# Score products of two heads (or of a differential head's two parts) issued in one step, in turn, each into a bank of its own

## The chip, the cores and the metric

The kernel runs on one core of one Trainium2 chip. The metric is the device time of one execution in microseconds, the median of three runs. A core has five engines that work through their own queues: PE (TensorE, matmuls; its weight loads are listed as PEld), DVE (VectorE), ACT (ScalarE), POOL (GpSimd) and SP, which only issues transfers here.

## What is computed

Three blocks in a row on x [256 tokens, 1024]: a block with a Fourier mixer, a convolution and 16 experts; a block with two attentions (eight heads with a compressed, a selected and a window branch, and eight plain causal heads); and two layers of four four-head mixers, each with a feed-forward part. The change concerns attention scores alone. Cut to those:

```python
# block 2: selected and window branch of nsa_attention, then moba_attention (256 tokens: causal, with ALiBi)
s = jnp.einsum('bgpqd,bgkd->bgpqk', qc, kwin) * scale - sl * dist
p = masked_softmax(s, mask)
o_win = jnp.einsum('bgpqk,bgkd->bgpqd', p, vwin)
# block 3, per layer: neighborhood, dilated and differential attention (latent attention has no pairs here)
s = jnp.einsum('bqhd,brqchd->bqhrc', q_row, k_nb) * scale + bias
s = jnp.einsum('bqhcd,bkhcd->bchqk', q_blk, k) * scale + bias[None, None]   # c: the two parts of a differential head
p = jax.nn.softmax(s, axis=-1)
a = p[:, 0] - lam * p[:, 1]
```

All sums are in float32. Heads are 64 wide, the parts of a differential head 32.

## The kernel before

The big products (`proj`, `proj_piece`, lines 147 to 149) have the tokens as stationary operand and 512 weight columns as moving one. A weight is split into a rounded part (ACT, line 99) and a rest (DVE, line 100), and three products per 128 rows, each in one pass, go into a bank of the pool `mm`. A projection keeps two of that pool's five banks, one for each half of the tokens, until ACT or DVE has read them.

The attentions are side work: generators that `pump` runs by a step or, with `rate` 2, by two steps between pieces of the projections. `pipeline` makes a step of three things: the score products and softmax of item i (`st1`), the transposes of the probabilities of item i - 2 (`st2`, lines 1077 and 1372), and the products with v of item i - 3 (`st3`, lines 1092, 1094, 1398, 1546). An item is one head, in block 2 one head of one branch, in the differential mixer one part of a head.

In `st1` of block 2 `scores` takes a bank of `mm`, makes the two causal halves (128 queries by 128 keys, line 1055; 128 queries by 256 keys, line 1056) and the softmax on them: DVE adds the bias and takes the maximum (line 1061), ACT the exponential (1065), DVE scales (1070). In the mixers `qk` (line 1360) makes two products of 128 queries by 256 keys, and `softmax` follows (1344 to 1354). The operands of a score product lie on 64 partitions: those of an even head on 0 to 63, those of an odd one on 64 to 127. A differential head's two parts lie on 32 partitions each. So two heads that follow each other use different rows of the PE array, but in this kernel their products stand in different steps.

A scheduler fixes the order of each engine's instructions when the program is built, and a tile waits for a free buffer of its pool.

Of the kernel before, what the change touches and what calls it, by code (L numbers as in the profile page):

```python
# [29 lines left out]
def row_bc(src, n):  # L30
    """A [n] DRAM vector seen by all partitions."""
    return bass.AP(src.tensor, src.offset, [[0, P], [1, n]])


class Net:
# [28 lines left out]
    def hT(self, tag, dt=F32R):  # L64
        """One of the two [128, 8, 256] tiles that carry a phase's transposed input."""
        return self.hp.tile([P, 2048], dt, tag=tag, name=tag).rearrange("p (k t) -> p k t", t=S)
# [4 lines left out]
    def load(self, dst, src):  # L71
        """The loads on this queue go out in the order that they are written down in."""
# [6 lines left out]
    def slot(self, dt=F32):  # L79
        """The next tile of the loads' rings."""  # L80
        pool, tag = self.rings[self.ring_at % len(self.rings)]
        self.ring_at += 1
        return pool.tile([P, 2064 if tag == "a8" else 2048], dt, tag=tag, name="wr")

    def load_rows(self, src):
        """The rows of src [k * 128, n] as [128, k tiles, n], in loads of up to 2048 columns; yields (first k tile, view)."""
# [15 lines left out]
    def behind(self, ins):  # L102
        """The next weights that are split wait on DVE behind ins."""
        self.held = [ins] * 3

    def split_to(self, t, raw):
        """Weights split into the two halves of a tile."""
# [15 lines left out]
    def proj(self, xh, xl, loads, n, evac, ahead=0):  # L123
        """out[half][128, n] = sum over k; loads are (first k tile, raw view [128, k tiles, n]). The first half of the rows
        takes the last pieces, ahead in number, before the second one does."""
# [27 lines left out]
    def queued(self):  # L153
        """The products of this block go out behind the last one that was noted, whichever is ready first."""
# [3 lines left out]
    def table(self, func, after):  # L158
        """Has the activation function's table in place before the data is; after [128, 1] is the last user of another one."""
        self.nc.scalar.activation(self.cp.tile([P, 1], F32, tag="warm", name="warm"), after, func)  # L160

    # Side work goes between the pieces of the projections: generators, run a step at a time in order.
# [4 lines left out]
    def soon(self, f):  # L167
        """Ahead of the other side work: one such closure per step."""
# [8 lines left out]
    def step(self):  # L177
        """A step of the first task, and of the next ones while the steps are light."""
# [7 lines left out]
    def finish(self, gen=None):  # L186
        """Emits side work up to the end of gen, or all of it."""
# [5 lines left out]
    def proj_cols(self, xh, xl, w, c0, n, evac, ahead=0):  # L193
        """Column chunk [c0, c0 + n) of a weight."""
# [9 lines left out]
    def rstd(self, ms, n, d, name, pool=True):  # L204
        """(ms / d + eps) ** -0.5 on [128, n] sums of squares: a power on Pool, or Newton steps on DVE where Pool is busy."""
# [11 lines left out]
        # Newton steps r (3 - t r r) / 2, with the factors -1/2 put off to the end  # L217
# [7 lines left out]
    def sumsq(self, x, n, name, ss=None):  # L225
        """Sums of squares over the last axis of x [128, 2, n], into ss [128, 2]."""
# [7 lines left out]
    def transpose_to(self, src, kts, consume, k0=0):  # L234
        """src [128 tok, 2, kts * 128] -> consume(kt, n, bank [128, n, 256]) for pairs of kt from k0 on."""
# [29 lines left out]
    def input_T(self, gain, name):  # L265
        """The residual stream as the next phase's input: its rows' rstd, and x^T * gain split in two, by column
        halves as they come. The rows' rstd is applied to the products, not to x."""
# [12 lines left out]
class InputT:  # L280
# [6 lines left out]
    def columns(self, c, soon=False):  # L287
        """Column half c; soon: its transposes go between the next projection's pieces."""
# [18 lines left out]
def gate_row(N, dst, src, j0, off):  # L307
    """dst[p, :] = mod[off:off + 1024] for every p, from column tiles j0, j0 + 1 of src, plus b_ada."""
# [10 lines left out]
def block1(N, stop):  # L319
    nc, a, tc = N.nc, N.a, N.tc  # L320
    x = N.x
    with ExitStack() as ctx:
# [29 lines left out]
        def ada_out(g, acc):  # L352
            """acc: rows 0, 32, 64, 96 hold the four 512-column blocks of c @ w_ada's group g."""
# [10 lines left out]
        def ada(g):  # L364
            """Weighted sum of the k tiles first, in steps that go between the projections, then one sum over partitions."""
# [38 lines left out]
        def shift_scale(c):  # L404
            """Shift and scale for k tiles 4 c .. 4 c + 3, a load per step, then the block's input with them."""
            accs, sbs, pt = [N.bank(N.po), N.bank(N.mm)], [], N.bank(N.tr)

            def columns(i):
                # the four partial sums, rows 0, 32, 64 and 96 of columns, become one column of rows
# [37 lines left out]
        # the first two chunks take their first k tiles while the second half of shift and scale is on its way  # L447
# [128 lines left out]
        for c in range(2):  # L576
            cc = slice(c * 512, c * 512 + 512)

            def ev(h, p, cc=cc):
# [7 lines left out]
                # the router's input, as it comes  # L587
# [8 lines left out]
class Router:  # L596
    """softmax(h2 @ w_router + b_router) with h2 = x * rstd * (g (1 + scale)) + shift: the affine part goes into the
    weights and a bias row, rstd onto the products."""
# [31 lines left out]
    def gate_rows(self):  # L630
        """gate_f's two halves on the partitions that hold them in the experts' outputs."""
# [7 lines left out]
    def squares(self, c, h):  # L639
        """Column half c of a half of the rows."""  # L640
# [31 lines left out]
    def second(self):  # L672
        """In an order in which the tensor engine has work while the last columns of x come."""
# [18 lines left out]
def moe(N, stop):  # L692
    nc, a, tc = N.nc, N.a, N.tc
    x, ident, rt = N.x, N.ident, N.router
    with ExitStack() as ctx:
        pool = ctx.enter_context(tc.tile_pool(name="moe1", bufs=1))
        N.m2 = ctx.enter_context(tc.tile_pool(name="m2m", bufs=1))
        # the ring goes on, with block 1's row tiles put in where they are free
# [29 lines left out]
        # the CAP largest are replaced, of equal ones the first; slots count up in order of index, 0 means not chosen  # L728
# [16 lines left out]
        # the chosen rows of x * rstd, exact in two parts, transposed; then the affine part of h2  # L745
# [29 lines left out]
        def out(n):  # L775
            """x + gate_f * moe for a column half: its sums of squares, the next input, then x = that * g_final and its sums."""
# [1015 lines left out]
```

## Time and profile before

| | |
|---|---|
| median of 3 runs | 2105.45 us |
| lowest, highest | 2105.32, 2109.12 us |
| the profiled execution, first to last instruction | 2108.0 us |
| block 2's eight heads with branches | about 1264 to 1340 us |
| block 2's eight plain heads | about 1364 to 1405 us |
| mixers of the two layers | about 1478 to 1573 us and 1807 to 1905 us |

The profile has no time for the execution besides its span, 2108.0 us. It gives the busy time of each engine by slice and by window, the chain of waits that ended last, groups of instructions by line, and the instructions in order of time. A PE record holds the pipeline's latency, so records overlap: what a product costs is the distance from its start to the next one's. A float32 product leaves two records (two passes), a product of the projections one.

### The profile page before, as it was taken

How to read it: one execution, taken by the hardware profiler on the slowest of the kernel's cores; microseconds unless marked ns; L12 is line 12 of the kernel's file. 1: busy time of each engine (PE TensorE's matmuls, PEld its weight loads, DVE VectorE, ACT ScalarE, POOL GpSimd, SP SyncE). 2: the span in 40 equal slices, each digit the busy share in tenths (PEclk: the TensorE clock that was granted, in tenths of full speed). 3: DMA queues.
4: the chain of work that ended last, by engine and by line, in shares of the span. 5: the costliest groups of instructions: out<-in, count | busy, mean ns of one | idle time of the engine just before them, and what ended most of it. 6: DMA issues, size and time to landing. Idle time of an engine off the chain costs nothing.

```text
span 2108.0 us, 22814 instructions
## 1 busy us (share of the span) xinstructions
PE 1756.7 (83%) x8895; PEld 1002.8 (48%) x8895; DVE 819.4 (39%) x1563; ACT 603.7 (29%) x1074; POOL 181.9 (9%) x135
## 2 busy tenths in 40 slices
PE   7989786566666666666666899999999999999998
PEld 4767631110110111111100487777778888778886
DVE  4797610000000000000000356676775545786554
ACT  4545410000000000000000345445545445455443
POOL 0671100000000000000000131112010000110000
PEclk9999897877777777766777899999999999999999
DMA  9879699999999999999999773336325556516551
GB/s 363 351 287 348 242 386 422 422 423 422 421 424 424 421 422 423 422 423 420 424 424 423 281 275 120 130 124 210 123 94 183 180 180 207 162 52 198 193 171 70
DMA packets 174396, 616.02 MB, mean 292 GB/s; under 512 B 11336, under 2 KB 20744, under 8 KB 139216
## 3 DMA queue, kind: packets, MB, share of 16 engines
q1 hardware_dynamic: 170288, 601.21, 73.4%
q0 software_dynamic: 3568, 12.75, 1.9%
q8 instruction: 70, 1.15, 0.2%
q10 hardware_dynamic: 432, 0.60, 0.1%
q14 instruction: 38, 0.31, 0.0%
HBM read 613.45 MB, written 4.24 MB: 293 GB/s over the span
## 4 chain that ended last, share of the span: by engine, by line
PE 51%; DMA 41%; DVE 5%; ACT 1%; issue 1%; POOL 0%; POOLq 0%; SPq 0%; DVEq 0%; ACTq 0%
DMA wr<-w_gate_e_dram 14%; DMA wr<-w_up_e_dram 14%; PE pb L147 13%; PE pb L148 13%; PE pb L149 13%; DMA wr<-w_down_e_dram 13%; PE pb L814 2%; DVE wl L100 2%; PE pb L242 2%; PE pb L1360 2%; PE pb L1372 1%; PE po L1398 1%; PE pb L760 1%; PE pb L1056 0%; PE pb L1055 0%
## 5 line engine op out<-in xcount | busy, mean ns | idle before, releaser
L100 DVE TENSOR_TENSOR wl<-wr,wh 128x1024 fp32r<-128x1024 f32 (+1 forms) x380 | 416.3, 1106 | 259.5 <-ACT wh L99 258.8
L814 PE MATMUL pb<-wr,XT 128*32 128x512 f32 x2048 | 362.8, 801 | 183.2 <-DMA wr<-w_up_e_dram 108.6
L99 ACT CAST wh<-wr 128x1024 fp32r<-128x1024 f32 (+1 forms) x380 | 340.0, 897 | 337.0 <-PE pb L149 313.1
L147 PE MATMUL pb<-wh,hh 128*128 128x512 f32 (+3 forms) x992 | 392.2, 396 | 1.8 <-ACT wh L99 1.2
L148 PE MATMUL pb<-wl,hh 128*128 128x512 f32 (+3 forms) x992 | 379.7, 383 | 6.6 <-DVE wl L100 6.5
L149 PE MATMUL pb<-wh,hl 128*128 128x512 f32 (+3 forms) x992 | 379.3, 383 | 0.0
L814 PEld LDWEIGHTS pb<-wr,XT 128*32 128x32 f32 x2048 | 47.9, 122 | 480.7 <-DMA wr<-w_up_e_dram 273.9
L857 PE MATMUL pb<-wr,hT 128*32 128x512 f32 x1024 | 186.7, 807 | 90.4 <-DMA wr<-w_down_e_dram 82.9
L828 DVE TENSOR_TENSOR hs<-pb,hs 128x512 f32<-128x512 f32 x16 | 11.1, 692 | 573.7 <-PE pb L814 573.7
L147 PEld LDWEIGHTS pb<-wh,hh 128*128 128x128 f32 x992 | 189.7, 191 | 50.0 <-issue 12.7
L148 PEld LDWEIGHTS pb<-wl,hh 128*128 128x128 f32 x992 | 189.8, 191 | 43.4 <-DVE wl L100 11.3
L149 PEld LDWEIGHTS pb<-wh,hl 128*128 128x128 f32 x992 | 189.3, 191 | 34.7
L827 ACT ACTIVATE hs<-pb 128x512 f32<-128x512 f32 x16 | 9.6, 598 | 543.9 <-PE pb L814 543.9
L857 PEld LDWEIGHTS pb<-wr,hT 128*32 128x32 f32 x1024 | 30.4, 127 | 229.3 <-DMA wr<-w_down_e_dram 194.6
L860 DVE TENSOR_TENSOR Y<-pb,gfr 128x512 f32<-128x512 f32 (+1 forms) x17 | 11.8, 692 | 269.1 <-PE pb L857 269.1
L841 ACT COPY Sc<-pb 128x256 f32<-128x256 f32 x16 | 6.0, 373 | 324.8 <-PE pb L839 324.8
L788 POOL TENSOR_TENSOR x<-x,grow 128x512 f32<-128x512 f32 x4 | 5.1, 1285 | 913.0 <-ACT jk L231 913.0
L147 PE MATMUL pb<-wh,ah 128*128 128x512 f32 x176 | 69.9, 397 | 0.0
L148 PE MATMUL pb<-wl,ah 128*128 128x512 f32 x176 | 69.6, 395 | 0.0
L149 PE MATMUL pb<-wh,al 128*128 128x512 f32 x176 | 69.6, 395 | 0.0
L864 PE MATMUL acc<-Y,Sc 64*128 64x512 f32 x128 | 45.9, 813 | 15.3 <-DVE Y L860 15.3
L1353 ACT ACTIVATE sb<-sb,cm 128x256 f32<-128x256 f32 x64 | 32.1, 503 | 40.5 <-DVE cm L1350 40.5
(505 smaller groups left out, 1794.3 us busy)
## 6 DMA issues: line engine op xcount, KB each, us to landing
wr<-w_gate_e_dram SPq DMA_DIRECT2D x128, 1024.0 KB, 19.6
wr<-w_up_e_dram SPq DMA_DIRECT2D x128, 1024.0 KB, 19.7
wr<-w_down_e_dram SPq DMA_DIRECT2D x128, 1024.0 KB, 19.6
wr<-w_in_dram SPq DMA_DIRECT2D x62, 1024.0 KB, 7.9
wr<-w_ada_dram SPq DMA_DIRECT2D x24, 1024.0 KB, 12.2
wr<-w_gate_dram SPq DMA_DIRECT2D x22, 1024.0 KB, 5.1
wr<-w_up_dram SPq DMA_DIRECT2D x22, 1024.0 KB, 5.1
wr<-w_down_dram SPq DMA_DIRECT2D x20, 1024.0 KB, 5.0
```

Of the source, the lines that this page charges most:

```text
L99: self.nc.scalar.copy(hi, src)
L100: self.nc.vector.tensor_tensor(lo, src, hi.bitcast(F32), ALU.subtract)
L147: nc.tensor.matmul(o, xh[:, kt, tok], hv[:, k, :], start=kt == first, stop=False)
L148: nc.tensor.matmul(o, xh[:, kt, tok], lv[:, k, :], start=False, stop=False)
L149: self.last_mm = nc.tensor.matmul(o, xl[:, kt, tok], hv[:, k, :], start=False, stop=kt == last).ins
L242: self.nc.tensor.transpose(pv[:, j, h * P:(h + 1) * P], src[:, h, (k + j) * P:(k + j + 1) * P], self.ident)
L760: nc.tensor.matmul(pg, part[:, h, k * P:(k + 1) * P], G[:, h, es].rearrange("p e c -> p (e c)"), start=(h == 0 and i == 0), stop=(h == 1 a ...
L814: N.last_mm = nc.tensor.matmul(pacc[32 * j:32 * j + 32, :], XT[:, k + kk, e, :], wt[:, kk, j * 512:(j + 1) * 512], start=(k + kk == 0), st ...
L857: nc.tensor.matmul(py[32 * q:32 * q + 32, :], hT[:, b, 32 * j:32 * j + 32], wt[:, i, n * 512 - c0:n * 512 - c0 + 512], start=(j == 0 and b ...
L864: nc.tensor.matmul(acc[n][h], Sc[r, h * P:(h + 1) * P], Y[r, :], start=(e == 0), stop=(e == NE - 1))
L1353: nc.scalar.activation(sb[:, c], (ps if bias is None else sb)[:, c], AF.Exp, bias=mm[:, h:h + 1], accum_out=sm[:, h:h + 1])
L1360: nc.tensor.matmul(ps[:, h * S:(h + 1) * S], q[:, h * P:(h + 1) * P], k, start=True, stop=True, tile_position=tile_position)
```

## The change

`scores` and `qk` take the operands of two items. They take a bank for each and issue the first product of the one, the first of the other, then the second of each. In block 2 the product with 256 keys now stands first. `st1` of an even item makes the products of the pair and keeps both banks; the odd item's step finds its scores there and only does the softmax. The latent mixer, whose heads lie on partitions 0 to 95 alone, keeps one head at a time. Comments were taken out too, so line numbers shift.

```diff
-        def scores(q, k, bias, gate):
-            ps = N.bank(N.mm)
-            nc.tensor.matmul(ps[:, :P], q[:, :P], k[:, :P], start=True, stop=True)
-            nc.tensor.matmul(ps[:, P:384], q[:, P:], k, start=True, stop=True)
+        def scores(heads):
+            ps = [N.bank(N.mm) for _ in heads]
+            for p, (q, k) in zip(ps, heads):
+                nc.tensor.matmul(p[:, P:384], q[:, P:], k, start=True, stop=True)
+            for p, (q, k) in zip(ps, heads):
+                nc.tensor.matmul(p[:, :P], q[:, :P], k[:, :P], start=True, stop=True)
+            return ps
+
+        def softmax(ps, bias, gate):
...
-                self.sb[i] = scores(self.q(n), self.k(s, n), self.bias[j], self.gate and self.gate(s, n))
+                if j == 0:
+                    self.ps[i], self.ps[i + 1] = scores([(self.q(m), self.k(s, m)) for m in (n, n + 1)])
+                self.sb[i] = softmax(self.ps.pop(i), self.bias[j], self.gate and self.gate(s, n))
...
-        def qk(q, k, tile_position=None):
-            ps = N.bank(N.mm)
+        def qk(*heads):
+            ps = [N.bank(N.mm) for _ in heads]
             for h in range(2):
-                nc.tensor.matmul(ps[:, h * S:(h + 1) * S], q[:, h * P:(h + 1) * P], k, start=True, stop=True, tile_position=tile_position)
+                for p, (q, k, *pos) in zip(ps, heads):
+                    nc.tensor.matmul(p[:, h * S:(h + 1) * S], q[:, h * P:(h + 1) * P], k, start=True, stop=True,
+                                     tile_position=pos[0] if pos else None)
             return ps
...
-                sb, sm = softmax(qk(*qk_of(n)), bias and bias(n))
+                if n % together == 0:
+                    for m, ps in enumerate(qk(*(qk_of(n + m) for m in range(together)))):
+                        pss[n + m] = ps
+                sb, sm = softmax(pss.pop(n), bias and bias(n))
...
-                sms[i] = softmax(qk(tv(df[0])[r, n // 2, :], tv(df[1])[r, n // 2, :], (r.start, 0)), tb[:, n])
+                if c == 0:
+                    pss[i], pss[i + 1] = qk(part(i), part(i + 1))
+                sms[i] = softmax(pss.pop(i), tb[:, n])
```

What moves on PE, first in block 2, at a step of an odd head. The rows name a line, the bank written (`pb`, `po`), the operands read (`wh`, `wl` a weight's two parts, `hh`, `hl` the input's, `sb` probabilities, `kT`, `qa` keys and queries) and the output's shape. Before, the odd head's scores stand between the transposes and the projection:

```order
L149 MATMUL pb<-wh,hl 128x512
L1077 MATMUL pb<-ident,sb 128x128 x3
L1055 MATMUL pb<-kT,qa 128x128
L1056 MATMUL pb<-kT,qa 128x256
L147 MATMUL pb<-wh,hh 128x512
```

The same step after the change:

```order
L149 MATMUL pb<-wh,hl 128x512
L1084 MATMUL pb<-ident,sb 128x128 x3
L147 MATMUL pb<-wh,hh 128x512
L148 MATMUL pb<-wl,hh 128x512
L149 MATMUL pb<-wh,hl 128x512
```

The odd head's two score products have left this place. They now stand at the even head's step (lines 1099 and 1101 are the products with v), which reads:

```order
L149 MATMUL pb<-wh,hl 128x512
L1099 MATMUL po<-pT,vr 64x256 x2
L1101 MATMUL po<-pT,vr 64x128 x2
L1084 MATMUL pb<-ident,sb 128x128 x3
L1057 MATMUL pb<-kT,qa 128x256 x2
L1059 MATMUL pb<-kT,qa 128x128 x2
L147 MATMUL pb<-wh,hh 128x512
```

There each score line stands twice, once per head and bank, where it stood once before. The second place is the differential mixer of the first layer, on PE (`df` are its queries and keys, `mr` the latent mixer's values). Before, two parts stand in two steps:

```order
L242 MATMUL pb<-ident,rows 128x128 x4
L1398 MATMUL po<-pT,mr 64x256 x4
L1360 MATMUL pb<-df 128x256 x2
L1372 MATMUL pb<-ident,sb 128x128 x4
L1360 MATMUL pb<-df 128x256 x2
L147 MATMUL pb<-wh,hh 128x512
```

After the change:

```order
L242 MATMUL pb<-ident,rows 128x128 x4
L1411 MATMUL po<-pT,mr 64x256 x4
L1371 MATMUL pb<-df 128x256 x4
L1384 MATMUL pb<-ident,sb 128x128 x4
L147 MATMUL pb<-wh,hh 128x512
```

The two parts' four products stand in a row, and one place where score products begin and end is gone. Over the whole program the score products of block 2 stand at 12 places in place of 24. In a layer, the differential mixer's stand at 4 in place of 9, the neighborhood's at 2 in place of 3, and the dilated mixer's at 3 in place of 4: its second pair stays apart, one head and then the other, as before.

## Rows read from the trace of the kernel before

**Rows 1.** The page's parts 1 (busy us by engine) and 4 (chain).

```profile
PE 1756.7 (83%) x8895; PEld 1002.8 (48%) x8895; DVE 819.4 (39%) x1563; ACT 603.7 (29%) x1074; POOL 181.9 (9%) x135
...
PE 51%; DMA 41%; DVE 5%; ACT 1%; issue 1%; POOL 0%; POOLq 0%; SPq 0%; DVEq 0%; ACTq 0%
```

**Rows 2.** Busy us by window: engine (instructions), granted clock, DMA share, GB/s.

```profile
1264.00:1340.00 76.00, 75.79 (x380) 53.98 (x378) 53.07 (x172) 39.56 (x93) 12.73 (x7) 1.00 0.34 111
1364.00:1405.00 41.00, 41.00 (x197) 28.55 (x196) 31.77 (x93) 19.40 (x47) 9.24 (x5) 1.00 0.34 116
1405.00:1420.00 15.00, 15.00 (x75) 12.11 (x75) 12.87 (x18) 7.34 (x9) 0.00 (x0) 1.00 0.50 148
...
1498.00:1543.00 45.00, 44.11 (x231) 33.56 (x230) 37.89 (x118) 22.24 (x60) 5.64 (x5) 0.94 0.24 77
1830.00:1875.00 45.00, 44.13 (x249) 33.59 (x249) 37.79 (x118) 23.37 (x64) 5.65 (x5) 1.00 0.24 77
```

**Rows 3.** Who PE waited for, 1265 to 1960 us: us in total, times, longest.

```profile
PE pb L1360 <- ACT sb L1353: 3.3, 2, 1.7
PE pb L242 <- DVE x L1236: 2.8, 1, 2.8
PE pb L1360 <- DVE rows L1417: 0.7, 2, 0.4
```

**Rows 4.** Timeline of PE in block 2, one head's scores: start, us, records.

```profile
1364.00 0.39 PE L149 MATMUL pb<-wh,hl 128*128 128x512 f32 x1
1364.32 0.49 PE L1055 MATMUL pb<-mk,mq 64*128 64x128 f32 x2
1364.64 0.59 PE L1056 MATMUL pb<-mk,mq 64*128 64x256 f32 x2
1365.17 0.50 PE L147 MATMUL pb<-wh,hh 128*128 128x512 f32 x1
1365.51 0.39 PE L148 MATMUL pb<-wl,hh 128*128 128x512 f32 x1
1365.74 0.39 PE L149 MATMUL pb<-wh,hl 128*128 128x512 f32 x1
```

**Rows 5.** Records of line 1055 in the whole trace: duration ns, first and last start.

```profile
L1055 PE MATMUL pb<-kT,qa x32: 272/322/373, 1269.9 to 1340.2; 64*128 64x128 f32 x32
...
L1055 PE MATMUL pb<-mk,mq x16: 272/322/373, 1364.3 to 1395.0; 64*128 64x128 f32 x16
```

**Rows 6.** Timeline of PE in the first layer's mixers: one part, 1.5 parts, two heads.

```profile
1508.53 1.12 PE L1360 MATMUL pb<-df 32*128 32x256 f32 x4
1509.58 0.66 PE L1372 MATMUL pb<-ident,sb 128*128 128x128 f32 x4
...
1522.28 1.13 PE L1360 MATMUL pb<-df 32*128 32x256 f32 x6
1523.34 0.33 PE L1372 MATMUL pb<-ident,sb 128*128 128x128 f32 x1
...
1528.32 1.14 PE L1360 MATMUL pb<-na 64*128 64x256 f32 x8
1529.39 0.39 PE L147 MATMUL pb<-wh,hh 128*128 128x256 f32 x1
```

**Rows 7.** Chain of waits, 1476 to 1575 us: start, us, what it was.

```profile
1532.24 0.69 DVE pT L1374
...
1533.68 2.14 DVE sb L1366 x2
1535.82 1.15 DVE cm L1350
1536.97 0.40 DVE rows L1417
```

**Rows 8.** Who DVE waited for, 1498 to 1543 us; and one window as in rows 2.

```profile
DVE cs L1354 <- ACT sb L1353: 2.4, 4, 1.2
DVE pT L1374 <- PE pb L1372: 2.0, 2, 1.4
DVE sb L1348 <- PE pb L1360: 1.9, 2, 1.1
...
1538.00:1543.00 5.00, 5.00 (x21) 4.26 (x20) 5.00 (x16) 1.72 (x7) 0.00 (x0) 0.50 0.00 0
```

More of the change, by code (lines that the diff above doesn't have):

```diff
@@ L1119, in __init__ @@
                 self.first, self.zT, self.yh, self.yl = first, zT, yh, yl
-                self.sb, self.pT, self.bias, self.po = {}, {}, {}, None
+                self.ps, self.sb, self.pT, self.bias, self.po = {}, {}, {}, {}, None
             def at(self, i):
@@ L1375, in P_T, with heads @@
             return pT
-        def heads(qk_of, v, bias, kt0):
-            sbs, pTs, bs = {}, {}, []
+        def heads(qk_of, v, bias, kt0, together=2):
+            pss, sbs, pTs = {}, {}, {}
             def st1(n):
-                if n == 0 and bias:
-                    bs.append(bias)
-                sb, sm = softmax(qk(*qk_of(n)), bias and bias(n))
+                if n % together == 0:
+                    for m, ps in enumerate(qk(*(qk_of(n + m) for m in range(together)))):
+                        pss[n + m] = ps
+                sb, sm = softmax(pss.pop(n), bias and bias(n))
                 scale_P(sb, sm)
@@ L1503, in latent @@
                 yield
-            yield from heads(lambda n: (qkT[:, 0, n, :], qkT[:, 1, n, :]), lambda n, k: vrow[:, k, n, :], None, 6)
+            yield from heads(lambda n: (qkT[:, 0, n, :], qkT[:, 1, n, :]), lambda n, k: vrow[:, k, n, :], None, 6, 1)
         g_mla = N.side(latent())
@@ L1517, in differential, with part @@
         def differential():
-            od, sms, pTs = [], {}, {}
+            od, pss, sms, pTs = [], {}, {}, {}
+            def part(i):
+                n, c = divmod(i, 2)
+                r = slice(64 * (n % 2) + 32 * c, 64 * (n % 2) + 32 * c + 32)
+                return tv(df[0])[r, n // 2, :], tv(df[1])[r, n // 2, :], (r.start, 0)
             def st1(i):
                 n, c = divmod(i, 2)
-                r = slice(64 * (n % 2) + 32 * c, 64 * (n % 2) + 32 * c + 32)
-                sms[i] = softmax(qk(tv(df[0])[r, n // 2, :], tv(df[1])[r, n // 2, :], (r.start, 0)), tb[:, n])
+                if c == 0:
+                    pss[i], pss[i + 1] = qk(part(i), part(i + 1))
+                sms[i] = softmax(pss.pop(i), tb[:, n])
                 if c:
```

## The prediction

> **What bounds the kernel now.** I read the chain of waits first, then the windows of the stretches where the change works, then who PE waited for, then single places. The chain is PE for 51% of the span, transfers for 41% and DVE for 5% [rows 1]; the transfers are the experts' stage, which the change doesn't touch. In block 2 PE is busy in 75.79 of 76, 41.00 of 41 and 15.00 of 15 us, with transfers at 34 to 50% of their engines and DVE at 70 to 86% [rows 2]. From there to the end of the mixers the longest waits of PE on another engine sum to 7 us in some 700 [rows 3]. So PE sets the pace: a microsecond taken from its queue there is taken from the kernel, until DVE, the next busiest, has no room left. The mixers are where that is close: DVE has 37.9 of 45 us in the first layer and 37.8 in the second [rows 2], and between 1532.2 and 1537.4 the chain runs through DVE, not PE [rows 7].
>
> **What one head's scores cost PE in block 2.** From line 149 at 1364.00 to line 148 at 1365.51 stand one 149, the scores and one 147 [rows 4]. Products of the projections follow each other by 0.23 (1365.74 less 1365.51). So a head costs 1.51 - 2 x 0.23 = 1.05 us. Two rows give what of it is passes and what is change of array shape. Let u be a pass of 256 keys, half of it one of 128, and c a change of shape, one way. Lines 1055 and 1056 have two passes each: 3u + 2c = 1.05. Where one part's scores go out alone in the mixers, four passes of 256 keys and the way back take 1509.58 - 1508.53 = 1.05 us [rows 6]: 4u + c = 1.05. So both are 0.21; I use u = 0.215 and c = 0.20, which fit both within the 0.01 of the starts: 0.65 us of passes and **0.40 us** of change. One sees the latter at the edges too: the first pass starts 0.09 after line 149's slot is over (1364.32 less 1364.23), and line 147 to 148 takes 0.34 in place of 0.23.
>
> **What a pair costs.** The trace of before already has pairs. Where one part's scores go out alone, four passes take 1.05 us up to the next line; where one and a half parts are adjacent, six passes take 1.06; where two heads of the neighborhood mixer are adjacent, eight take 1529.39 - 1528.32 = 1.07 [rows 6]. Twice the passes in the same time: neighbours on different rows run side by side, on 64 and on 32 partitions, even though these eight were issued as one head's two products and then the other's. So a pair costs what a head costs plus 0.02, and the removed call is worth its whole time. [...]
>
> **Block 2.** Line 1055 has 48 records, two per call [rows 5], so 24 calls; 12 go, and the odd steps go from transposes to projection without a change of shape. 12 x 1.05 = **12.6 us** of PE time. The weight load for a pass of 128 keys has only 0.11 us to hide in, and there are now two; if they didn't load side by side it would cost 2 x 0.11 per pair, 2.6 us in all. For 256 keys they do hide [rows 6], so I take nothing and keep the 2.6 for the range. DVE and ACT have the same instructions as before. The first head's softmax waits no longer, since the pair ends when the single head did; the second's scores lie ready. DVE needs 53.07 of 76 us and 31.77 + 12.87 of 56 [rows 2]; with 8.4 and 4.2 us less it would be at 79% and 86%. At the end of the second stretch it is tightest, and I take off 1.0 us. Left: **11.6 us**.
>
> **The mixers, per layer.** A pass of 256 keys is 0.215 us. Differential: eight calls of 0.86 less 0.43 already side by side are 6.45 us of passes; after, four pairs of 0.86, 3.44. Places fall from 9 to 4, five times 0.40. PE gains 3.0 + 2.0 = 5.0. Neighborhood: the first pair is side by side already; of the second, passes go from some 1.7 to 0.86 and one place goes: 1.3. Dilated: the first pair loses one call's passes, 0.86, and one of two shape changes, 0.2 (the products with v stand between its heads now, and after them later): 1.1. The second pair stays as it is, gain 0. PE's sum is **7.4 us** a layer.
>
> What DVE lets through is less. Differential and neighborhood lie in the 45 us windows, where DVE is busy 37.9 and waits 2.4 us for ACT's exponential [rows 2, 8]. Those 40.3 us stay; its waits for PE can go. At most 45 - 40.3 = 4.7 of 6.3 us can come out, and I take **4.0**, because the waits don't fall away evenly. The dilated 1.1 lies behind and counts in full. 5.1 a layer, **10.2** for two.
>
> **The sum.** 11.6 + 10.2 = 21.8 us. Against the profiled execution, 2108.0 - 21.8 = 2086.2, 1.03% less; the profile is 2.55 above the median of the runs, so **2083.7** for the median of 2105.45. The feed-forward parts and the experts have no edit and count 0: PE remains their pace or the transfers do.
>
> **The waits added.** A pair takes two of the five `mm` banks, and the second is held until the odd head's softmax one step later. A projection's next chunk needs two banks while its last two may still be read. PE's waits on a bank's reader are 0.7 us in two places now (line 1360 on the eviction at line 1417) [rows 3]. Behind such a wait stands the whole PE queue. I count 0, because between the odd step and the next chunk's second half there are several dense products, each 0.23.
>
> **The clock.** Between 1538 and 1543 the granted clock is 0.50, the lower of the two levels, after a stretch in which PE was waiting on DVE [rows 7, 8]. Such a stretch of 5 us does 2.5 us of full-speed work. Whether it stays, goes, or gets a twin in the second layer I can't read; it is 2.5 us to either side.
>
> **The rivals.** *All of PE's gain arrives.* DVE fills its waits exactly. 12.6 + 2 x 7.4 = 27.4, 2078.0. For it: DVE's queue is never full over a whole stretch in block 2. Against: the DVE chain in each layer.
>
> *DVE takes the stage.* DVE gives nothing in the 45 us windows and nothing in the plain heads' stretch of block 2. Left are the eight pairs with branches, 8.4 us, and the dilated 1.1 twice: 10.6, 2094.9. For it: 5.00 of 5 us from 1538 on and five microseconds of chain [rows 7, 8]. Against: DVE waited 3.9 us for PE in the same 45 us [rows 8]. [...]
>
> *No overlap in the new order.* Two banks in turn could behave unlike the old adjacency. Then only shape changes go: 12 and about 2 x 6.5 places of 0.40, 10.0 us, 2095.4. Against: rows 6.
>
> *Slower.* The held bank blocks the projection. 26 pairs now hold one; if each made PE wait w for the softmax of the odd head, the loss is 26 w, and from w = 0.84 us on it eats the 21.8. At 1.0 it gives 2105.45 + 4.2 = 2109.7. For it: a bank is freed by DVE, which is behind exactly where it is full. Against: the only such waits now are 0.35 us each.
>
> **How the numbers follow.** The forecast, PE's gain less what DVE holds back (2079 to 2089): 0.62. All of it, 2078 and a clock stretch less: 0.08. DVE takes the stage (2089 to 2097): 0.21. No overlap: 0.03. The change brings nothing because bank waits eat it: 0.03. Slower: 0.03. The range must hold 8 in 10: from 2077, all of PE's gain and 1 us of clock, to 2095, the DVE rival's time. 0.2%, 4.2 us, is about what a measurement of this kernel can tell from no change. Faster by more: 0.62 + 0.08 + 0.21 + 0.03 = 0.94; within: 0.03; slower: 0.03.
>
> **What would show it.** In the profile after, lines 1057 and 1059 with four and four records at 12 places, a pair 1.05 to 1.1 us from first start to the next dense product; 1371 with eight records at 14 places in 1.07 us; the span from 1264 to 1420 of before some 11 us shorter, each 45 us window about 41. Wrong if the eight records take 1.5 us or more (no overlap), if dense products show gaps before their first pass behind a pair (banks), or if PE's waits on DVE in the mixers grow by more than 4 us a layer (the DVE rival).

## The result, and the profile after

The median of the changed kernel is 2081.58 us (2080.22 to 2082.63) against 2107.28 us for the runs of the kernel before that were made beside it: a ratio of 0.9879, 95% interval 0.9865 to 0.9893. Timed once more, in the experiments, it was 2082.13 us and 0.9876 (0.9861 to 0.989). The forecast was 2083.7 us, 2077.0 to 2095.0, and faster: time and direction came as forecast. The gain is 25.7 us (25.1 when timed once more), where the sum had 21.8; part of the closeness of the times is the kernel before, which was 1.8 us slower in these runs than the median that the forecast started from.

The page of the changed kernel, parts 1 (busy us by engine) and 4 (chain of waits), to be held against [rows 1]:

```profile
PE 1734.1 (83%) x8895; PEld 982.7 (47%) x8895; DVE 812.1 (39%) x1563; ACT 601.2 (29%) x1074; POOL 174.6 (8%) x135
...
PE 47%; DMA 42%; DVE 7%; ACT 1%; issue 1%; POOL 0%; SPq 0%; POOLq 0%; DVEq 0%; ACTq 0%
```

As many instructions on each engine as before, and PE 22.6 us less busy. In the chain PE falls from 51 to 47% of the span and DVE rises from 5 to 7%: a part of what PE no longer sets, DVE sets.

The windows of the changed kernel between the same products as the first, second, fourth and fifth window of [rows 2] (busy us by engine with instructions, granted clock, DMA share, GB/s):

```profile
1261.03:1328.64 67.61, 67.42 (x378) 50.95 (x377) 52.05 (x170) 38.85 (x90) 8.20 (x6) 1.00 0.39 125
1352.65:1389.60 36.95, 36.95 (x197) 27.18 (x196) 30.41 (x92) 18.62 (x46) 6.74 (x5) 1.00 0.37 127
1482.25:1520.40 38.15, 36.53 (x231) 28.81 (x230) 34.29 (x112) 21.07 (x57) 5.64 (x5) 1.00 0.27 90
1805.04:1845.31 40.27, 38.73 (x250) 30.82 (x250) 36.30 (x119) 23.12 (x64) 5.64 (x5) 1.00 0.25 85
```

76 us have become 67.61, 41 have become 36.95: 8.4 us for eight pairs and 4.05 for four, and PE is as full as before. The 45 us of the mixers have become 38.15 and 40.27, and there PE now idles 1.62 and 1.54 us, where before it idled 0.89 and 0.87 [rows 2]. The granted clock of the first layer's window was 0.94; it is 1.00.

PE's timeline of the changed kernel: a pair in block 2, a pair of differential parts, a pair of neighborhood heads (start, us, records):

```profile
1352.64 0.39 PE L149 MATMUL pb<-wh,hl 128*128 128x512 f32 x1
1352.96 0.70 PE L1057 MATMUL pb<-mk,mq 64*128 64x256 f32 x4
1353.49 0.39 PE L1059 MATMUL pb<-mk,mq 64*128 64x128 f32 x4
1353.81 0.50 PE L147 MATMUL pb<-wh,hh 128*128 128x512 f32 x1
1354.15 0.40 PE L148 MATMUL pb<-wl,hh 128*128 128x512 f32 x1
...
1482.88 1.13 PE L1371 MATMUL pb<-df 32*128 32x256 f32 x8
1483.95 0.50 PE L147 MATMUL pb<-wh,hh 128*128 128x512 f32 x1
...
1508.80 1.13 PE L1371 MATMUL pb<-na 64*128 64x256 f32 x8
1509.87 0.39 PE L147 MATMUL pb<-wh,hh 128*128 128x256 f32 x1
```

The pair in block 2 costs 1354.15 - 1352.64 - 0.46 = 1.05 us, what one head cost [rows 4]. Eight passes of 256 keys take 1.07 us in either mixer (1483.95 - 1482.88 and 1509.87 - 1508.80), where four took 1.05 for a part alone [rows 6].

Who PE waited for in the changed kernel, 1262 to 1930 us (us in total, times, longest), to be held against [rows 3]:

```profile
PE pb L1371 <- ACT sb L1362: 3.2, 2, 1.6
PE pb L242 <- DVE x L1245: 2.8, 1, 2.8
PE pb L1384 <- DVE sb L1378: 2.4, 4, 0.9
PE pb L242 <- DVE orow L1575: 1.9, 2, 1.0
PE pb L1384 <- DVE sb L1549: 0.7, 2, 0.3
```

The first two are those of before. The wait for a bank (`rows`) is gone. New or longer are three waits for DVE, all in the mixers: the transposes of probabilities (line 1384) wait for `sb`, the scaled probabilities, and those of the differential result `orow` (line 242) for its norm. Before, the same transposes (line 1372) waited for `sb` alone, and less:

```profile
PE pb L1372 <- DVE sb L1366: 0.7, 3, 0.3
```

### The profile page after: what moved, and what is told of

It is laid out like the page before. It is cut to its first block, busy times and chain, and to the rows that moved or that the text cites. A ratio compares the mean times of both kernels' runs of the same rounds, so it can differ in the third digit from the quotient of the medians.

```text
span 2078.4 us, 22803 instructions
## 1 busy us (share of the span) xinstructions
PE 1734.1 (83%) x8895; PEld 982.7 (47%) x8895; DVE 812.1 (39%) x1563; ACT 601.2 (29%) x1074; POOL 174.6 (8%) x135
## 4 chain that ended last, share of the span: by engine, by line
PE 47%; DMA 42%; DVE 7%; ACT 1%; issue 1%; POOL 0%; SPq 0%; POOLq 0%; DVEq 0%; ACTq 0%
DMA wr<-w_gate_e_dram 14%; DMA wr<-w_up_e_dram 14%; PE pb L147 13%; PE pb L148 12%; PE pb L149 12%; DMA wr<-w_down_e_dram 12%; DVE wl L100 2%; PE pb L814 2%; PE pb L242 1%; PE pb L1371 1%; ACT sb L1362 1%; PE pb L857 1%; PE pb L1384 1%; PE pb L760 1%; PE po L1411 0%
## 5 line engine op out<-in xcount | busy, mean ns | idle before, releaser
L814 PE MATMUL pb<-wr,XT 128*32 128x512 f32 x2048 | 376.3, 828 | 167.7 <-DMA wr<-w_up_e_dram 92.2
L100 DVE TENSOR_TENSOR wl<-wr,wh 128x1024 fp32r<-128x1024 f32 (+1 forms) x380 | 414.4, 1101 | 259.3 <-ACT wh L99 258.2
L860 DVE TENSOR_TENSOR Y<-pb,gfr 128x512 f32<-128x512 f32 (+1 forms) x17 | 11.8, 691 | 269.9 <-PE pb L857 269.9
```

The costliest lines, as they stand in the source:

```text
L100: self.nc.vector.tensor_tensor(lo, src, hi.bitcast(F32), ALU.subtract)
L814: N.last_mm = nc.tensor.matmul(pacc[32 * j:32 * j + 32, :], XT[:, k + kk, e, :], wt[:, kk, j * 512:(j + 1) * 512], start=(k + kk == 0), st ...
```

## Where the time went, product by product

The products of the projections (lines 147 to 149, 3984 records) stand in the same order in every kernel here. So a stage can be cut at the same two products in each trace, and its lengths compared to 0.1 us. The cuts are, in the time of the profile before: block 2 from 1243.16 to 1430.84, the mixers of the layers from 1483.18 to 1588.34 and from 1806.59 to 1906.51. In brackets stands how long the granted clock was at 0.50, the lower level, in that stage. Score products are in pairs in all kernels where nothing else is said.

```
kernel                                   block 2   first layer     second layer
before                                    187.69   105.16 (6.8)     99.92 (3.4)
before, second trace (e9)                 187.74   106.50 (10.2)    98.66 (0)
changed                                   175.47    97.45 (0)       93.31 (0)
changed, second trace (e10)               175.39    97.26 (0)       94.03 (0)
e1  mixers as before                      175.45   104.63 (6.8)    102.46 (10.2)
e2  block 2 as before                     187.81    97.39 (0)       93.86 (0)
e3  head by head                          175.47    98.70 (0)       95.11 (0)
e4  second head on the same rows          183.18   100.12 (0)       96.17 (0)
e5  differential paired, others not       175.48    97.65 (0)       94.31 (0)
e6  others paired, differential not       175.48   104.94 (6.8)     98.30 (0)
e7  changed, copies on ACT                175.42    94.83 (3.4)     91.17 (3.4)
e8  before, copies on ACT                 187.69   100.33 (0)       97.73 (3.4)
e11 128 keys first in block 2             175.53    97.20 (0)       93.73 (0)
```

In the first two profiles (before, changed) the change gives 12.2 us in block 2, 7.7 in the first layer and 6.6 in the second, 26.5 in all. The spans differ by 29.6 (2108.0 less 2078.4); of the 3.1 left, 3.0 arise before block 2, where the kernels don't differ. The second trace of before has the experts 1.7 us longer and what stands ahead of them 2.9 us shorter than the first trace, so executions differ by that much there. In the first two profiles every clock record is 1.00 or 0.50. Between the cuts, right behind block 2, both have one more stretch at 0.50, of 6.8 us (before, from 1438.6) and 3.4 us (changed, from 1424.9), behind a wait of 2.76 us of PE for DVE: so it stands there with either order of the scores.

## The experiments

**One part of the change at a time.** In e1 the mixers keep one head at a time:

```diff
-        def heads(qk_of, v, bias, kt0, together=2):
+        def heads(qk_of, v, bias, kt0, together=1):
...
-                if c == 0:
-                    pss[i], pss[i + 1] = qk(part(i), part(i + 1))
+                pss[i], = qk(part(i))
```

> The change in block 2 alone; the mixers' score products are issued one head at a time as before. The trace after puts 12.2 us of its gain into block 2 (distance of the same dense products, before less after, grows from 2.97 to 15.18 us between 1243 and 1431 us of before). Theory: the twelve removed places are worth their whole 1.05 us each and do not depend on the mixers: about 12 us less than before, 0.994 of it, some 2094 to 2096 us. In the mixers the two stretches at the lower clock that the trace of before has (6.83 us from 1537.6 and 3.41 us from 1820.9) should be there again if the mixers' old order brings them about. Rival (the mixers' gain of the whole change rests on work that block 2 leaves earlier): more than 14 us. Rival (the low-clock stretches come and go by themselves, whatever the order): the trace of this kernel lacks one or both of them, or has them elsewhere, and the time can be up to 5 us lower.

Measured: 2096.51 us against 2108.27, ratio 0.994 (0.992 to 0.9961), 11.8 us. Block 2 is that of the changed kernel, and both layers show the lower clock, the second 10.2 us of it. In e2 block 2 goes back, `scores` for one head at each step and 128 keys first:

```diff
-                if j == 0:
-                    self.ps[i], self.ps[i + 1] = scores([(self.q(m), self.k(s, m)) for m in (n, n + 1)])
+                self.ps[i], = scores([(self.q(n), self.k(s, n))])
```

> The change in the mixers alone; block 2 issues one head at a time, 128 keys first, as before. Theory: TensorE gets 7.4 us a layer from removed places and side by side passes, DVE holds back about 2 us of it in each layer, so 5.1 to 5.5 a layer, 10.2 to 11 us in all; and if the low-clock stretches of the mixers go with the old order, up to 3.4 + 1.7 us more: 10 to 16 us, some 2092 to 2097 us. The gains of this kernel and of the one with block 2 alone should sum to that of the whole change, 25.7 us. Rival (DVE holds back nothing, the clock has no part): 14.8 us with DVE waits no longer than before. Rival (low-clock stretches by chance): 10 to 11 us against runs of before that have none, and the stretches seen in some trace of the new order too.

Measured: 2094.62 us, ratio 0.9935 (0.9917 to 0.9954), 13.7 us, and no lower clock in the mixers. The two gains sum to 25.4 us, and the whole change gave 25.7 and 25.1: within the intervals the parts add up. The traces say it more sharply, since each stage of e1 and e2 has the length that it has in the kernel with the same order there, but for the clock.

**In turn, or only adjacent.** e3 issues both products of the one head, then both of the other:

```diff
-            for h in range(2):
-                for p, (q, k, *pos) in zip(ps, heads):
+            for p, (q, k, *pos) in zip(ps, heads):
+                for h in range(2):
```

> The whole change, but without the turns: both products of the one head, then both of the other, still in one step and each head in its own bank. Theory: what counts is that neighbours in the queue lie on different rows; the trace of before has eight passes in 1.07 us in just this order. So a pair costs 1.05 us in block 2 and 1.07 in the mixers, and the time is that of the changed kernel within 1 us (2080.5 to 2083). Rival (passes start and end strictly in the order of the program): only the last pass of the one head and the first of the other overlap. A pair in block 2 then has 1.29 - 0.11 = 1.18 us of passes in place of 0.65, 12 x 0.53 = 6.4 us more; in the mixers 1.72 - 0.22 = 1.5 in place of 0.86, 0.64 us for each of 14 pairs, 9.0 more: 2090 to 2097 us.

Measured: 2086.19 us (0.9901, 0.9878 to 0.9924). Block 2 is the same to 0.01 us (175.47 in both), so there the turns bring nothing: neighbours on other rows run side by side in this order too, as the eight passes in 1.07 us of [rows 6] had it. A pair in block 2 of e3:

```profile
1355.44 0.71 PE L1057 MATMUL pb<-mk,mq 64*128 64x256 f32 x4
1355.98 0.40 PE L1058 MATMUL pb<-mk,mq 64*128 64x128 f32 x4
1356.30 0.50 PE L147 MATMUL pb<-wh,hh 128*128 128x512 f32 x1
```

In PE's queue one head's product of 128 keys (line 1058) stands ahead of the other head's product of 256 keys (line 1057). The records show the four passes of line 1057 first, and the eight passes take 0.86 us up to line 147, as in the changed kernel (0.85). The rival, with the passes strictly in the order of the program, had block 2 an estimated 6.4 us longer; it fell. The layers are 1.3 to 1.4 and 1.1 to 1.8 us longer than in the changed kernel's traces, which no theory had. The timeline of e3 shows why, at the second neighborhood pair of the first layer:

```profile
1518.75 0.70 PE L1370 MATMUL pb<-na 64*128 64x256 f32 x2
1519.70 0.55 PE L1383 MATMUL pb<-ident,sb 128*128 128x128 f32 x3 [0.25 <-DVE sb L1377]
1520.18 0.70 PE L1370 MATMUL pb<-na 64*128 64x256 f32 x2
1521.24 1.13 PE L1370 MATMUL pb<-na 64*128 64x256 f32 x4 [0.36 <-DVE rows L1429]
```

The pair has come apart: in the queue that the scheduler made, the first head's products stand between transposes, and the second head's come behind them and wait 0.36 us for their bank. That is one place more, 0.40 us, and 0.86 us of passes that no longer run side by side: an estimated 1.26 us a layer. No other pair of e3 that is whole in the changed kernel came apart. Issued in turn, the first head's second product stands behind the second head's first, which needs the second bank; the pair goes out whole, at 1516.76 in the changed kernel. The turns don't make the overlap, they keep the pair together.

**Rows or places.** In e4 the second of a pair reads the first's operands:

```diff
-                    self.ps[i], self.ps[i + 1] = scores([(self.q(m), self.k(s, m)) for m in (n, n + 1)])
+                    self.ps[i], self.ps[i + 1] = scores([(self.q(m), self.k(s, m)) for m in (n, n)])
...
-                    for m, ps in enumerate(qk(*(qk_of(n + m) for m in range(together)))):
+                    for m, ps in enumerate(qk(*(qk_of(n) for m in range(together)))):
...
-                    pss[i], pss[i + 1] = qk(part(i), part(i + 1))
+                    pss[i], pss[i + 1] = qk(part(i), part(i))
```

> The whole change, but the second of a pair takes the operands of the first, so both lie on the same rows; each still has its own bank, and the products are issued in turn. The odd head's (or part's) scores are left out by this: its output is that of the even one. What remains of the change is that a pair's products stand at one place. Theory: rows that differ are what lets passes run side by side, so a pair has 1.29 us of passes in place of 0.65 in block 2, 12 x 0.65 = 7.8 us more, and 1.72 in place of 0.86 in the mixers, 14 x 0.86 = 12.0 us more if TensorE sets the pace there, 2 us a layer less where DVE held it up anyway: 2097 to 2102 us, half to three quarters of the gain lost. A pair in block 2 takes 1.29 + 0.40 = 1.69 us. Rival (the bank decides, not the rows): within 2 us of the changed kernel, a pair at 1.05.

Measured: 2095.81 us (0.9944, 0.9926 to 0.9961), a little less than expected. PE's timeline of e4, a pair in block 2:

```profile
1362.73 0.39 PE L149 MATMUL pb<-wh,hl 128*128 128x512 f32 x1
1363.05 1.13 PE L1057 MATMUL pb<-mk,mq 64*128 64x256 f32 x4
1364.02 0.60 PE L1059 MATMUL pb<-mk,mq 64*128 64x128 f32 x4
1364.55 0.50 PE L147 MATMUL pb<-wh,hh 128*128 128x512 f32 x1
1364.88 0.39 PE L148 MATMUL pb<-wl,hh 128*128 128x512 f32 x1
```

1364.88 - 1362.73 - 0.46 = 1.69 us, in place of 1.05 on two sets of rows. Block 2 stands between the two kernels: 4.5 us below before, which is the places (0.38 for each of 12), and 7.7 above the changed kernel, which is the overlap (0.64 for each). The prediction's two numbers, 0.40 and 0.65, are measured apart here. In the layers 6.0 us of passes came back (seven pairs at 0.86) and cost only 2.8 and 2.5 against the mean of the changed kernel's two traces: the waits for DVE shrank, from 2.4 to 0.5 us for `sb` and from 1.9 to none for `orow`. So over half of that work cost nothing. 2.2 and 2.3 us of it filled time in which PE had idled (it idles 2.3 us in a layer of e4, and 4.5 and 4.65 in the changed kernel's); the rest, some 1.1 us a layer, isn't explained.

**Which mixer pays, and which brings the clock down.** e5 leaves the neighborhood and dilated heads apart (`together=1` alone), e6 the differential parts (`qk(part(i))` alone).

> Block 2 as changed; in the mixers only the differential parts are paired, the neighborhood and dilated heads are issued one at a time as before. Of TensorE's 7.4 us a layer the differential mixer has 5.0. Theory: the mixers of a layer are 4 to 5 us shorter than before, less what DVE holds back, and the lower clock is back where the neighborhood's single heads meet DVE's full stretch (6.83 us at about 1527 in the first layer), since in the traces so far it stands there with the old order (twice of two in the first layer) and not with the new one (no time in eight layers): mixers of the first layer 100 to 102 us in place of 97.4, the whole 2084 to 2090 us. Rival (the clock falls with the differential parts' single products): no stretch at the lower clock in the mixers and 98 to 99 us for the first layer.

> The counterpart: block 2 as changed, neighborhood and dilated heads paired, the differential parts one at a time as before. TensorE's gain is 1.3 + 1.1 = 2.4 us a layer, and DVE has fewer of TensorE's waits to lose. Theory (the neighborhood's single heads bring the clock down): no stretch at the lower clock in the neighborhood mixer, mixers of the first layer 100 to 101 us, of which 2.5 us against the old order are clock; the whole 2084 to 2090 us. Rival (the differential parts bring it down): a stretch of 3.4 us or more at the lower clock stays in each layer, mixers 102 us and more.

Measured: e5 2081.98 us (0.9896, 0.9881 to 0.9911), e6 2094.69 us (0.9955, 0.9939 to 0.9971). My theory fell at both: without pairs of neighborhood and dilated heads the layers are 97.65 and 94.31 us, within 0.3 and 0.6 us of the mean of the changed kernel's two traces, and the clock stays up; with them alone the first layer is as long as before, with the lower clock, and the second, without it, is 98.30 us where e9's is 98.66. In e6 PE waits 2.0 us for banks (`rows`), 0.7 before [rows 3] and not at all in the changed kernel:

```profile
PE pb L1371 <- DVE rows L1430: 2.0, 2, 1.0
PE pb L242 <- DVE orow L1574: 1.6, 2, 0.8
```

Nearly the whole gain of the mixers is that of the differential parts; of what the other pairs take from PE, waits take most back.

**DVE's share.** e7 and e8 are the changed kernel and the one before with a copy moved:

```diff
-            nc.vector.tensor_copy(pT, pt)
+            nc.scalar.copy(pT, pt)
```

> The changed kernel, but in the mixers the copy of the transposed probabilities (0.60 us, sixteen a layer) is made by ACT in place of DVE. In the trace of the changed kernel TensorE waits 2.5 us a layer for DVE there (sb L1378 1.2, orow 1.0, sb L1549 0.3). Theory (DVE holds back 2 to 2.5 us of TensorE's 7.4 us a layer): with 9.6 us a layer less on DVE these waits go, and the mixers of a layer are 2 to 3 us shorter: 94.5 to 95.5 us in the first, 2076 to 2079 in all. Rival (the waits are latency from one engine to the next, not DVE's load): within 1 us of the changed kernel. Rival (ACT becomes the pace, its exponentials stand behind the copies): mixers longer than 97.4.

> The kernel before with the same copies on ACT. Theory: TensorE sets the pace of the old mixers nearly everywhere, so DVE's relief brings little by itself, under 1 us a layer; but if DVE's full stretch ahead of the neighborhood mixer's end is what lets the clock fall, the 6.83 us at the lower clock of the first layer go and give 2.5 to 3 us more: 2100 to 2107 us against 2108. Then the gain of the change between the two kernels with ACT copies is 12.2 in block 2 and close to TensorE's whole 7.4 a layer, 25 to 27 us, without a part for the clock. Rival (the lower clock comes from the order of the score products, whatever DVE does): the stretches stay, 104 to 105 us in the first layer.

Measured: e7 2077.01 us (2076.07 to 2077.69; 0.987, 0.9854 to 0.9887), by the ratio not to be told from the changed kernel (0.9879). But e5, whose layers are within 0.6 us of the changed kernel's, was timed in the same round, and its executions (2080.97 to 2083.57) all lie above those of e7. The layers of e7, and who PE waited for there:

```profile
1469.24:1564.07 94.83, 91.45 (x515) 70.82 (x513) 72.95 (x215) 62.54 (x150) 6.63 (x6) 0.98 0.34 114
1782.76:1873.93 91.17, 87.81 (x491) 67.76 (x489) 70.66 (x201) 55.96 (x136) 10.51 (x6) 0.98 0.34 113
```

```profile
PE pb L1384 <- DVE sb L1378: 2.8, 4, 0.9
PE pb L242 <- DVE x L1245: 2.8, 1, 2.8
```

The layers are 2.5 us shorter than the mean of the changed kernel's two traces, and the wait for `orow` is gone; the one for `sb` has stayed. The wait for `orow` is 1.0 us of the 2.5. Moving the copy also changed PE's own queue: the products of the probabilities with v (line 1411) stand at 4 places a layer for the neighborhood and dilated heads where they stood at 7, and PE's busy time fell too, by 1.1 to 1.5 us a layer in spite of the clock. So e7 is no clean measure of DVE's share. That the wait for `orow` came from what else DVE had to do there fits it but isn't shown by it alone; that for `sb` has another cause, which stays open. e8 is 2101.26 us, ratio 0.9988 (0.9971 to 1.0005): not clear of no change over its executions, which reach from 2098 to 2111, though its trace has a first layer of 100.33 us without the lower clock. Between e8's and e7's second layers, both with 3.4 us of lower clock, lie 6.6 us: more than the 5 between the changed kernel and the one before, and short of PE's 7.4.

**Second traces, and the order of the products.** e9 is the kernel before, e10 the changed one, e11 has the loops over 128 and 256 keys in the other order.

> The kernel before once more, for a second trace of it. Question: do the stretches at the lower clock in the mixers belong to the old order or to one execution? So far the layers with the differential parts apart have them in six of eight cases (4.5 us on average where there are any counts as 3.4 to 10.2 us a layer), the layers with the parts paired and the copies on DVE in none of ten. Theory (they belong to the old order): at least one of the two layers has a stretch of 3.4 us or more; first layer 104 to 105.5 us with 6.8 us of it, second 98.5 to 102.5. Rival (they belong to single executions): none in either layer, first layer about 102.5, second about 98.7.

> The changed kernel once more, timed in five rounds against the kernel before, for the size of the gain and a second trace. Theory: 0.987 to 0.989 of before; mixers 97.3 to 97.7 and 93.2 to 94.3 us, no stretch at the lower clock in them; block 2 as in the first trace within 0.1 us. Rival (the missing stretches were chance): one of 3.4 us or more in a layer, that layer 1.3 to 2.5 us longer.

> The changed kernel with the product of 128 keys first in block 2, then that of 256, each still of the two heads in turn. Question: whether the weights' load behind a pass of 128 keys (0.11 us) shows, which the prediction left in its range with 0.22 us a pair. In the changed kernel a pair takes 1.05 us with the 256 keys first, no more than one head did with the 128 keys first. Theory (the loads of the two heads hide behind each other's passes in either order): stretch of the eight pairs with branches 102.2 us, as the changed kernel, time within 1 us of it. Rival (the order was chosen rightly, a short pass hides no load): 0.1 to 0.2 us for each of 12 pairs, 0.8 to 1.8 us more in that stretch.

Measured: e10 as said above; e11 2082.65 us (0.9882, 0.9865 to 0.9898), with block 2 0.06 to 0.14 us longer: the order of the two products costs about 0.01 us a pair, so no load of weights shows in either. e9's layers, by windows between the cuts of the table:

```profile
1484.17:1590.68 106.51, 103.73 (x515) 76.70 (x514) 80.55 (x230) 54.33 (x134) 6.36 (x6) 0.95 0.31 101
1808.93:1907.59 98.66, 95.46 (x492) 70.32 (x489) 78.90 (x217) 47.60 (x120) 10.22 (x6) 1.00 0.32 106
```

The first layer has more of the lower clock than in the first trace, the second none: an old layer at full clock, 98.66 us, which the rival had put at 98.7.

## Why the prediction was right

**What a head and a pair cost.** Right to 0.02 us, in both parts: 0.40 us for the change of shape and 0.65 for the passes out of two rows, 0.38 and 0.64 by e4; a pair at 1.05 and 1.07.

**Block 2.** 11.6 us were forecast and 12.2 came. The step that was off is the 1.0 taken away for DVE at the end of the plain heads: only 0.2 to 0.4 of the 12.6 are missing (12.2 to 12.35 came). That DVE holds these isn't shown: between the plain heads and the end of the attentions PE waits for no engine before the 2.8 us for `x`, which the kernel before has too.

**DVE in the mixers.** PE's busy time and idle time of a layer, in windows between the table's cuts, before:

```profile
1483.18:1588.34 105.16, 102.22 (x514) 75.75 (x513) 80.92 (x231) 54.37 (x134) 6.37 (x6) 0.97 0.31 103
1806.59:1906.51 99.92, 97.04 (x491) 71.52 (x489) 78.64 (x217) 47.77 (x120) 10.24 (x6) 0.98 0.31 104
```

and after:

```profile
1467.85:1565.30 97.45, 92.94 (x515) 69.76 (x513) 79.68 (x231) 54.05 (x134) 6.37 (x6) 1.00 0.34 111
1783.55:1876.86 93.31, 88.87 (x491) 66.77 (x489) 74.96 (x217) 47.41 (x120) 11.05 (x6) 1.00 0.33 113
```

PE idled 2.94 and 2.88 us in a layer and idles 4.51 and 4.44: it loses 1.6 us more a layer to waits, where I had let DVE keep 2.3 of 7.4. At one clock the second layers of e9 and e10 differ by 4.6 us; with the first trace of the changed kernel it is 5.35, so about 5.0 against the forecast's 5.1. The size was right; the place was not. Followed along those two layers, the distance grows by 4.7 us in the differential and neighborhood mixers, all that I had called possible (I took 4.0). It grows by 1.1 more at the dilated pair, and then falls by 1.2. The step that failed is "The dilated 1.1 lies behind and counts in full". Four microseconds further PE waits, in the changed kernel's timeline:

```profile
1526.71 1.13 PE L1371 MATMUL pb<-dl 64*128 64x256 f32 x8
...
1530.99 0.66 PE L242 MATMUL pb<-ident,orow 128*128 128x128 f32 x4 [0.98 <-DVE orow L1575]
```

The norm of the differential result is a chain of small DVE instructions that stand between splits of 1.2 us and other heads' softmax, here on DVE:

```profile
1528.04 0.16 DVE L220 SCALAR_TENSOR_TENSOR r_q<-r_q,r_t 128x8 f32<-128x8 f32 x1
1528.11 1.22 DVE L100 TENSOR_TENSOR wl<-wr,wh 128x1024 fp32r<-128x1024 f32 x1
1529.25 0.16 DVE L221 SCALAR_TENSOR_TENSOR r_r<-r_q,r_r 128x8 f32<-128x8 f32 x1
...
1530.24 0.69 DVE L1575 TENSOR_TENSOR orow<-orow,r_r 128x512 f32<-128x512 f32 x1
```

PE, arriving earlier, gets there before it. In e5, where the dilated heads are not paired, PE doesn't wait for `orow` at all: the wait takes back what the dilated pair gives. I had looked for DVE's hold only in windows where DVE is full; here a chain of dependent instructions held PE up behind them too, 0.98 us.

**The clock.** I set it to zero in the sum, with 2.5 us to either side; it was the largest term that I missed. The trace of before had 3.4 us of it in the second layer too, from 1820.9, ahead of the window that I read [rows 2]. The old second layer has three traces with the same code and 0, 3.4 and 10.2 us of lower clock: 98.66 (e9), 99.92 (before), 102.46 us (e1). That is 0.37 us for each microsecond of it, from three single executions, not 0.5; probably PE would have waited for part of that time. By this, 2.5 us of the first layer's 7.7 and 1.3 of the second's 6.6 in the two profiles are clock, which leaves 5.2 and 5.3 for the rest. So the forecast's terms without the clock came out at 12.2 + 5.2 + 5.3 = 22.7 us against 21.8, and the 3.8 of clock are a gain that no step of the sum had. With the copies on DVE the lower clock goes with the order: of eight layers with the differential parts apart (before, e1, e6, e9) six have it, of fourteen with them paired none. With the copies on ACT it doesn't: one of two layers apart has it (e8), and both of the paired ones (e7). The times agree: in the round of e1 to e4 the kernels with the parts apart spread by 11 us (e1, 8 executions) and 12 us (before, 15 executions), those with them paired by 4 to 5 (e2, e3 and e4, 4 to 6 executions). One place where it fell, in e1's timeline:

```profile
1833.91 1.12 PE L1371 MATMUL pb<-df 32*128 32x256 f32 x4
1834.96 0.33 PE L1384 MATMUL pb<-ident,sb 128*128 128x128 f32 x1
1835.22 0.69 PE L1371 MATMUL pb<-df 32*128 32x256 f32 x2
1835.85 0.55 PE L1384 MATMUL pb<-ident,sb 128*128 128x128 f32 x3
1836.33 1.21 PE L1371 MATMUL pb<-df 32*128 32x256 f32 x2
1837.47 0.79 PE L147 MATMUL pb<-wh,hh 128*128 128x512 f32 x1
```

From 1836.4 the clock is 0.50 for 6.8 us. PE didn't wait here: for 2.5 us, from 1833.91 on, it had run nothing but single parts' products, on 32 rows, and transposes. It fell at this same place, with no idle time of PE in the 6 us before, in three more traces: e9 (1518.7) and e6 (1504.5) in the first layer and e8 (1841.8) in the second. So four of ten layers with the parts apart have a fall there, and none of sixteen with them paired, where the place doesn't exist. Other falls came behind a wait: at 1537.6 of before [rows 7], at 1820.9 after 1.7 us of waiting for ACT. In e7 the clock falls once a layer with the parts paired, for 3.4 us, in the first layer behind waits of 0.51 and 0.89 us ahead of the second neighborhood pair; in the changed kernel PE waits 0.88 us there and it doesn't fall. That the single parts' products bring about one kind of fall fits these four places and e5 against e6, but why it fell in four layers and not in the other six isn't shown; what decides behind a wait stays open.

**The rivals.** "All of PE's gain arrives" is nearer by the gain (27.4 against 25.7 measured, the forecast 21.8) and further by the time, but it came another way: PE's waits grew, and the clock filled the gap. "DVE takes the stage" is false for the stage and true for two mixers: pairing the neighborhood and dilated heads brings at most 0.6 us a layer of their 2.4 (e5). e7, with DVE's copies of the transposed probabilities moved to ACT and 2.5 us a layer gained, fits it in the mixers. Block 2 shows no such bound: PE is busy there in 67.42 of 67.61 us. "No overlap" falls with the pair at 1.05 us, where e4 on the same rows has 1.69; "slower" falls with the waits: none for a bank is left. A pool of fewer banks was not tried.

## What to carry to other kernels

Here a small product with few rows among full ones cost its passes and 0.40 us for going in and out of its shape; put next to one on other rows, both costs of the second were gone (a pair took 1.05 us, one head 1.05). Issue interleaved what the scheduler may pull apart: one pair of e3 that came apart cost an estimated 1.26 us a layer. Count the gain where the engine behind has room, and follow the chains of small dependent instructions that the faster engine will now meet early, not only the full windows. And look at the granted clock: here some stretches at 0.50, of 3.4 and 6.8 us, went with the old order, and in the two profiles that gave an estimated 3.8 us on top of the products' time.

## What was not expected of the hardware

In e3's block 2, four passes on one set of rows and four on another ran side by side though the queue has all of one before the other: 0.86 us for the eight of a pair, and 0.85 in the changed kernel's. And the granted clock fell to 0.50 while PE was busy without a gap, behind single parts' products on 32 rows, in four traces (e1, e6, e8, e9) at the same place of the program, for 3.4 or 6.8 us.
